# Half products in the last group of the down projection, and one first load for norm weights and x

## The chip, the cores and the metric

The kernel runs on one core of a Trainium2 chip. Its time is in device microseconds, as the median of several executions. A core has TensorE (matmuls; PE in the profile), VectorE (DVE), ScalarE (ACT), GpSimd (POOL) and SyncE (SP). SP, ACT and POOL also issue DMAs; a DMA that POOL issues can add what it carries to what stands at its destination. "PEld" is TensorE's loading of a weight tile, "PEclk" the clock that the chip grants to TensorE.

## The reference

One decoder layer over 512 tokens of width 1024 in float32: a pooling mixer and a sparse attention side by side, joined by gates, then a feed-forward network with a causal convolution of width 3. Cut to what matters here:

```python
h = rms_norm(x, mix_norm_g)
proj = h @ w_in                                     # u, q, kv, gates
# kv's first two slots go, block by block, into compressed keys and values:
blk = kv[:, idx] + pe                               # additive position weights
hid = silu(einsum('bnlgd,ldh->bngh', blk, w1));  kc = hid @ w2
x = x + (gate_pool * y_pool + gate_nsa * y_nsa) @ w_out
h = rms_norm(x, ffn_norm_g)
gate_pre, val = split(h @ w_up)                     # 2 x 2816 features
y = silu(causal_dwconv(gate_pre, conv_w, conv_b)) * val
x = x + y @ w_down                                  # 2816 -> 1024
```

## The kernel before

Activations stand transposed, 128 features in the partitions and 512 tokens along the row. A float32 matrix product is made of three matmuls: each operand is split into a rounded high part and a low remainder (`split`: ScalarE copies the high part, VectorE subtracts; `split_by_dma` leaves the subtraction to a POOL DMA that adds), and high x high, high x low and low x high are summed in a PSUM bank (`mm3`).

The order is not written out. Every operation is recorded by `Plan.note`, with what it reads and writes. `Plan.emit` then tries several orders with rough costs of its own, and issues the best: each engine's queue in the order found. TensorE's own order is that of the program, in two streams that are interleaved during the attention. `pl.behind(op)` holds an operation back until another one is done; `soon` tiles are handed out in the order of the program. Recorded operations all carry the line at which `emit` issues them, so the profile names nearly everything L394; tiles tell what an instruction is.

Tiles are drawn from a common set of 54 pages of 512 columns (`page`), from rings of three for raw and split weights (`wraw`, `whi`, `wlo`, 1024 columns each) and from PSUM banks (`mm`, `tr`, `av`, `sc`); `any_bank` walks over them.

The stages that the change touches:

- **The head.** `first` loads the first weights `wa[0]` in two parts over SP's queue, and between them the first half of the first x tile; ScalarE's queue loads sixteen columns of the parameters (`pr`, among them the norm weights `mixg`) and then the other half of x. ScalarE scales x by the norm weight into `xh`. Until then TensorE runs nine warm-up matmuls on ones. The remaining parameters come after the second round of this stage.
- **Compression.** `kv_in` makes `kc`, and VectorE adds the position weights to give `kcb`; these additions are `behind(turned[3])`, the last operation that is recorded for the last of the four transposed query and key tiles (`qk_transpose`: TensorE transposes, ScalarE and VectorE copy into `qt` and `kt`). TensorE multiplies `kcb` with `w1`, and the result goes as `hid` into a small matmul with `w2`.
- **The up projection** runs over 22 features f, each a gate and a value tile. Features 0 and 2 are made plainly (`up_plain`), the others by `up_fast`: the four blocks of output (gate and value by two halves of 256 tokens) come from seven half products instead of eight, on sums of weights and of activations (`product`, twelve matmuls of 256 columns each). The last two products of a feature are `held` and run within the next one.
- **The down projection** is in groups of four features of y. When four are ready (`AT`), a group puts eight blocks of twelve matmuls of 512 columns on a list (`dn_group`), and `FILL` says how many of them each later feature takes between its products (`fill`). What is left runs after the last feature. Its sums stay in `x2`.
- **The last group** takes the six features y[16] to y[21]: for each of the eight output tiles f, weights `wdz[f]` (768 columns), eighteen matmuls of 512 columns, an addition of `x2[f]` and the output. The last tile goes in two halves of 256 tokens.

```python
    for f in range(8):
        wh, wl = weights(flat(wdz[f]), 768, "v")
        pt = any_bank()
        o = page("o")
        if f < 7:
            mm3(pt, wh, wl, yh, yl, 16, KF, koff=16, nk=KF, first=16)
            DVE.tensor_add(o, pt, x2[f])
            SP.dma_start(out[f], o)
            continue
        # the last tile: the same in two halves of 256 tokens
```

Of the kernel before, what the change touches and what calls it, by code (L numbers as in the profile page):

```python
# [57 lines left out]
FILL.update({18: (0, 1, 0, 0), 19: (0, 1, 0, 0), 20: (0, 1, 0, 0), 21: (0, 1, 0, 0)})  # L58
# [339 lines left out]
def hybrid_layer(ctx: ExitStack, tc: tile.TileContext, xT, pos, par, cst, poolw, w1, wa, wb, wf,  # L398
# [71 lines left out]
    pr = keep("pr", (P, NPAR))  # L470
    ps_i = keep("ps_i", (P, 5), I32)
# [17 lines left out]
    mixg = R("mixg")  # L489

    POOL.memset(ones, 1.0)
    ACT.dma_start(pr[:, 0:16], par[:, 0:16])
    pt = bank("mm")
    for i in range(9):
        PE.matmul(pt[:, 0:P], ones, ones, start=(i == 0), stop=(i == 8))
# [7 lines left out]
    H2 = T // 2  # L503

# [4 lines left out]
    def first():  # L509
        raw, hi, low = ring("wraw"), ring("whi", F32R), ring("wlo", F32R)  # L510
        xr[0] = page("xr")
# [8 lines left out]
        DVE.tensor_copy(hi[:, :T], raw[:, :T])  # L520
        for c in cuts:
# [53 lines left out]
    for k in range(KD):  # L575
# [12 lines left out]
        if k == 1:  # L588
            SP.dma_start(ps_i, pos)
            SP.dma_start(cs, cst)  # L590
            SP.dma_start(pr[:, 16:], par[:, 16:])
# [110 lines left out]
    def qk_transpose(t):  # L702
# [7 lines left out]
        if t % 2:  # L710
            pt = bank("tr", (P, 2, 2, P))
            with pl.unit():
                for j in range(2):
                    for b in range(2):
                        PE.transpose(pt[:, j, b], kp[t - 1 + j][:, 2 * b:2 * b + 2].rearrange("p a d -> p (a d)"), ident)
            for g in range(2):
# [8 lines left out]
    turned = []  # L725
# [20 lines left out]
    with pl.on("f"):  # L746
        def kv_in(i):
# [417 lines left out]

    def split_y(f, y):
        yh[f], yl[f] = page("yh", dt=F32R), page("yl", dt=F32R)
        split(yh[f], yl[f], y)

# [26 lines left out]
    def product(bank_, a, b, k0):  # L1196
        ah, al = a
        bh, bl = b
        for k in range(4):
            c = slice(k * P, (k + 1) * P)  # L1200
            with pl.unit():
                for j, (w, x) in enumerate(((ah, bh), (ah, bl), (al, bh))):
                    PE.matmul(back(bank_[:, :H2]), w[:, c], back(x(k)), start=k0 and k == 0 and j == 0,
                              stop=k == 3 and j == 2, skip_group_check=True)
# [41 lines left out]
    def up_fast(f, n1, n2, n3):  # L1246
        rg, r1, r2 = ring("wraw"), soon("r1"), soon("r2")
        SP.dma_start(rg, flat(wup[f, 0]))
        with pl.behind(begun[-2 - max(0, 3 - f)]):
            SP.dma_start(r1, flat(wup[f, 1, :, 0:4]))  # L1250
            SP.dma_start(r2, flat(wup[f, 1, :, 4:8]))

        def pair():
            return soon("sh", F32R), soon("sl", F32R)

        def summed(x):
            lo, hi = soon("sl", F32R), soon("sh", F32R)
            split_by_dma(hi, lo, x)
            return hi, lo

        a1 = ring("whi", F32R), ring("wlo", F32R)
        split(*a1, rg)
        halves_ = lambda a, i: tuple(q[:, i * 512:(i + 1) * 512] for q in a)
        s3 = soon("s3")
        DVE.tensor_add(s3, rg[:, :512], r1)
        h5 = summed(r2)
        DVE.tensor_add(r1, r1, r2)
        h3 = summed(s3)
        DVE.tensor_add(rg[:, :512], rg[:, :512], r1)
        h1 = summed(r1)  # L1270
        h2 = pair()
        split(*h2, rg[:, :512])
        DVE.tensor_add(rg[:, 512:], rg[:, 512:], rg[:, :512])
        h4 = summed(rg[:, 512:])
# [4 lines left out]
        product(bx, halves_(a1, 0), mov(0, 0), True)  # L1279
# [16 lines left out]
        product(bx, halves_(a1, 1), mov(1, 0), False)  # L1296
# [32 lines left out]
    for f in range(8):  # L1329
# [3 lines left out]
        if f < 7:  # L1333
            mm3(pt, wh, wl, yh, yl, 16, KF, koff=16, nk=KF, first=16)
            DVE.tensor_add(o, pt, x2[f])
            SP.dma_start(out[f], o)
            continue
        for h in range(2):
            s = slice(h * H2, (h + 1) * H2)
            pt = any_bank() if h else pt  # L1340
            for k in range(16, KF):
                c = slice((k - 16) * P, (k - 15) * P)
                with pl.unit():
                    for j, (w, q) in enumerate(((wh, yh), (wh, yl), (wl, yh))):
                        PE.matmul(back(pt[:, :H2]), w[:, c], back(q[k][:, s]), start=k == 16 and j == 0,
                                  stop=k == KF - 1 and j == 2)
            DVE.tensor_add(o[:, s], pt[:, :H2], x2[f][:, s])
            SP.dma_start(out[f, :, s], o[:, s])
# [4 lines left out]
_INS = ["xT", "pos", "par", "cst", "poolw", "w1", "wa", "wb", "wf", "wpo", "wno", "wout", "wup", "wdn", "wdz"]  # L1353


def _layout(x, positions, mix_norm_g, w_in, q_norm_g, k_norm_g, cmp_pe, cmp_w1, cmp_w2, pool_w,
# [30 lines left out]
    A["par"] = np.concatenate([par[n] for n in PAR], axis=1)  # L1387
    q, kk = np.arange(P)[:, None], np.arange(P)[None, :]
# [55 lines left out]
```

## Time and profile before

| | |
|---|---|
| median of 3 runs | 691.0 us (690.94 to 691.12) |
| profiled execution | 690.67 us, its span 688.9 us |
| TensorE, its weight loads | 683.1 us (99%), 606.0 us (88%) |
| VectorE, ScalarE, POOL | 502.6 (73%), 430.0 (62%), 100.2 (15%) |
| granted clock | 1.0 throughout |
| moved by DMA | 113.99 MB, 165 GB/s on average |

Times in the profile count from the span's start. A timeline's row gives start, duration, engine, operation, what it writes and reads, the count, and in brackets the idle time before it with what ended it. Matmuls overlap: the duration of one (0.39 us for 512 columns) is longer than the distance to the next. A group's row gives the count, busy time and the mean in ns of one, and idle time; a DMA group's row the size and the median from issue to landing. A row of a stretch gives its length and then for TensorE, weight loads, VectorE, ScalarE and POOL the busy time and (count), then the granted clock, the share of the DMA engines and GB/s.

### The profile page before, as it was taken

The page shows a single profiled execution, that of the slowest core. Times are in us where ns is not written, and L with a number is a line of the kernel's source. Part 1 is how long each engine was busy: PE and PEld are TensorE (multiplying, and loading weights), DVE is VectorE, ACT ScalarE, POOL GpSimd, SP SyncE. Part 2 cuts the span into 40 slices and gives each one's busy share as a digit, 9 for nine tenths or more (in the row PEclk, how much of TensorE's full clock was granted, in tenths as well). Part 3 has the DMA queues.
Part 4 walks back from the last instruction along what each step waited for, and adds up shares of the span by engine and source line. Part 5 has one row for each costly group of instructions (what it writes and reads, how often), then busy time and mean ns, then how long its engine had stood idle before and what let it go on. Part 6 is the DMA issues. An engine that isn't in the chain of part 4 may idle for free.

```text
span 688.9 us, 11345 instructions
## 1 busy us (share of the span) xinstructions
PE 683.1 (99%) x4126; PEld 606.0 (88%) x4126; DVE 502.6 (73%) x1093; ACT 430.0 (62%) x781; POOL 100.2 (15%) x126
## 2 busy tenths in 40 slices
PE   9999999999999999999999999999999999999997
PEld 8898888888888888888898999999999999999976
DVE  6868678887877644768868978677778777786642
ACT  7667477776776653346778866666567656675320
POOL 0011210111111110001123332122213222211000
PEclk9999999999999999999999999999999999999999
DMA  8468653545545557844778889677668667765131
GB/s 301 143 165 264 154 121 94 139 100 145 154 123 154 153 138 246 279 148 154 209 167 221 199 180 218 154 199 184 153 170 185 170 157 194 170 167 115 47 130 61
DMA packets 46279, 113.99 MB, mean 165 GB/s; under 512 B 5392, under 2 KB 6160, under 8 KB 46224
## 3 DMA queue, kind: packets, MB, share of 16 engines
q1 hardware_dynamic: 29808, 76.43, 32.5%
q0 software_dynamic: 16128, 36.71, 29.9%
q8 instruction: 32, 0.52, 0.3%
q14 instruction: 23, 0.19, 0.1%
q10 hardware_dynamic: 288, 0.14, 0.1%
HBM read 70.27 MB, written 6.29 MB: 111 GB/s over the span
## 4 chain that ended last, share of the span: by engine, by line
PE 97%; DVE 1%; DMA 1%; ACT 0%; issue 0%; SPq 0%
PE mm L394 37%; PE tr L394 33%; PE sc L394 16%; PE av L394 11%; DMA wraw<-wa 1%; ACT kt L394 0%; DVE ft L394 0%; DVE fg L394 0%; DVE wlo L394 0%; ACT ft L394 0%; SPq L394 0%; DVE yl L394 0%; DVE kcb L394 0%; DVE u L394 0%; DVE kt L394 0%
## 5 line engine op out<-in xcount | busy, mean ns | idle before, releaser
L394 ACT ACTIVATE whi<-wraw 128x1024 fp32r<-128x1024 f32 (+2 forms) x94 | 95.2, 1015 | 65.8 <-PE mm L394 26.7
L394 DVE TENSOR_TENSOR wlo<-wraw,whi 128x1024 fp32r<-128x1024 f32 (+1 forms) x66 | 76.2, 1156 | 4.6 <-ACT whi L394 4.2
L394 PE MATMUL mm<-xh,whi 128*128 128x512 f32 x176 | 72.3, 411 | 0.1
L394 PE MATMUL tr<-tl,sh 128*128 128x256 f32 x250 | 70.4, 282 | 0.0
L394 PE MATMUL mm<-xh,wlo 128*128 128x512 f32 x176 | 68.9, 392 | 0.0
L394 PE MATMUL mm<-xl,whi 128*128 128x512 f32 x176 | 68.9, 391 | 0.0
L394 PE MATMUL tr<-th,sl 128*128 128x256 f32 x240 | 67.7, 282 | 0.0
L394 PE MATMUL tr<-th,sh 128*128 128x256 f32 x240 | 67.5, 281 | 0.0
L394 PE MATMUL mm<-gh,whi 128*128 128x256 f32 (+1 forms) x320 | 60.8, 288 | 0.0
L394 POOL DMA_DIRECT2D wlo<-wraw x28 | 24.3, 867 | 238.3 <-ACT wlo L394 182.0
L394 POOL DMA_DIRECT2D sl<-r x40 | 34.5, 862 | 134.2 <-ACT sl L394 98.0
L394 PEld LDWEIGHTS mm<-gh,whi 128*128 128x128 f32 x320 | 49.5, 188 | 0.6
L394 PEld LDWEIGHTS tr<-tl,sh 128*128 128x128 f32 x250 | 47.0, 188 | 0.5
L394 PE MATMUL sc<-yh,whi 128*128 128x512 f32 x120 | 46.7, 389 | 0.0
L394 PE MATMUL sc<-yl,whi 128*128 128x512 f32 x120 | 46.7, 389 | 0.0
L394 PE MATMUL sc<-yh,wlo 128*128 128x512 f32 x120 | 46.7, 389 | 0.0
L394 PEld LDWEIGHTS tr<-th,sh 128*128 128x128 f32 x240 | 45.2, 188 | 1.2
L394 PE MATMUL mm<-gh,wlo 128*128 128x256 f32 (+1 forms) x160 | 45.9, 287 | 0.0
L394 PEld LDWEIGHTS tr<-th,sl 128*128 128x128 f32 x240 | 45.1, 188 | 0.0
L394 DVE SCALAR_TENSOR_TENSOR ft<-fg,pr,ft 128x511 f32<-128x511 f32 (+1 forms) x44 | 32.9, 749 | 14.3 <-ACT ft L394 13.7
L394 PEld LDWEIGHTS mm<-xh,wlo 128*128 128x128 f32 x176 | 33.0, 188 | 7.5
L394 ACT ACTIVATE u<-tr 128x256 f32<-128x256 f32 x40 | 15.3, 384 | 36.8 <-PE tr L394 24.2
(380 smaller groups left out, 1927.2 us busy)
## 6 DMA issues: line engine op xcount, KB each, us to landing
wlo<-wraw POOLq DMA_DIRECT2D x28, 512.0 KB, 4.7
wraw<-wup SPq DMA_DIRECT2D x24, 512.0 KB, 3.6
wraw<-wf SPq DMA_DIRECT2D x22, 512.0 KB, 3.4
r<-wup SPq DMA_DIRECT2D x40, 256.0 KB, 3.5
sl<-r POOLq DMA_DIRECT2D x40, 256.0 KB, 4.0
wraw<-wdn SPq DMA_DIRECT2D x16, 512.0 KB, 3.7
sl<-s POOLq DMA_DIRECT2D x20, 256.0 KB, 4.3
sl<-wraw POOLq DMA_DIRECT2D x20, 256.0 KB, 4.3
```

Source lines behind the costliest of these rows:

```text
L394: getattr(self.real[o.eng], method)(*a, **kw)
```

## The change

Four edits:

1. **The last group.** Output tiles 0 and 1 stay plain. Tiles 2 to 7 go in pairs (f, e) through `dz_fast`: seven products, each of three k x three matmuls of 256 columns, for two tiles by two halves of tokens. `y_sums` makes the sums and differences of y that this needs, for k = 16 to 18 with k + 3, when y[k + 3] is there. `half_weights`, taken out of `up_fast`, makes the sums of weights, at width 384 here. Three of its five halves are split with a POOL DMA, two by VectorE. `dz_plain` is the loop's body as it was.
2. **The fills.** `FILL` takes none of the blocks within features 19, 20 and 21; the three run after the last feature, in front of the last group.
3. **Compression.** The additions of `kcb` are behind the last transposition of keys on TensorE instead of behind the last copy of the tile.
4. **The head.** A new input `xa` has the sixteen parameter columns in front of the first x tile. ScalarE's queue loads the parameters and the first half of x in one DMA, SP's the second half. x and `mixg` then lie in `x0`, in the space that `ptc` takes later. `xl` is made in two halves; there are eight warm-up matmuls; the parameters are loaded whole later.

```diff
-FILL.update({18: (0, 1, 0, 0), 19: (0, 1, 0, 0), 20: (0, 1, 0, 0), 21: (0, 1, 0, 0)})
+FILL.update({18: (0, 1, 0, 0), 19: (0, 0, 0, 0), 20: (0, 0, 0, 0), 21: (0, 0, 0, 0)})
...
+    x0 = pl.tile(sb, (P, 4, T), F32, "x0", "ptc", 1).rearrange("p a t -> p (a t)")
...
-    mixg = R("mixg")
+    mixg = x0[:, 48:56]
...
-    ACT.dma_start(pr[:, 0:16], par[:, 0:16])
+    ACT.dma_start(x0[:, 48:64 + H2], xa[:, :16 + H2])
...
-    for i in range(9):
+    for i in range(8):
...
             SP.dma_start(raw[:, :T], wa[0, :, :T])
-            SP.dma_start(xr[0][:, cuts[0]], xT[0, :, cuts[0]])
+            SP.dma_start(xr[0][:, cuts[1]], xa[:, 16 + H2:])
             SP.dma_start(raw[:, T:768], wa[0, :, T:768])
-        ACT.dma_start(xr[0][:, cuts[1]], xT[0, :, cuts[1]])
...
-        DVE.scalar_tensor_tensor(xl[0], xr[0], mixg[:, 0:1], f32(xh[0]), op0=ALU.mult, op1=ALU.subtract)
+        for c in cuts:
+            with pl.behind(cast):
+                DVE.scalar_tensor_tensor(xl[0][:, c], xr[0][:, c], mixg[:, 0:1], f32(xh[0][:, c]), op0=ALU.mult,
+                                         op1=ALU.subtract)
...
-                with pl.behind(turned[3]):
+                with pl.behind(flipped[1]):
...
+    def y_sums(k):
+        b1, b2 = ylast[k], ylast[k + 3]
+        ta, tb = page("ta"), page("tb")
+        DVE.tensor_sub(ta[:, :H2], b1[:, :H2], b1[:, H2:])
+        DVE.tensor_sub(tb[:, :H2], b2[:, H2:], b1[:, H2:])
+        DVE.scalar_tensor_tensor(ta[:, H2:], ta[:, :H2], -1.0, b2[:, H2:], op0=ALU.mult, op1=ALU.subtract)
+        DVE.scalar_tensor_tensor(tb[:, H2:], ta[:, H2:], -1.0, b2[:, :H2], op0=ALU.mult, op1=ALU.subtract)
+        for i, x in ((0, ta), (1, tb)):
+            yth[k - 16, i], ytl[k - 16, i] = page("yth", dt=F32R), page("ytl", dt=F32R)
+            split(yth[k - 16, i], ytl[k - 16, i], x)
...
+    def half_weights(first, second, w, dma, gate):
+        rg, r1, r2 = ring("wraw"), soon("r1"), soon("r2")
+        SP.dma_start(rg[:, :2 * w], first)
+        with pl.behind(gate):
+            SP.dma_start(r1[:, :w], second[0])
+            SP.dma_start(r2[:, :w], second[1])
...
+        a1 = tuple(ring(n, F32R)[:, :2 * w] for n in ("whi", "wlo"))
+        split(*a1, rg)
+        s3 = soon("s3")[:, :w]
+        DVE.tensor_add(s3, rg[:, :w], r1)
+        h5 = parts(r2, dma[0])
+        DVE.tensor_add(r1, r1, r2)
+        h3 = parts(s3, dma[1])
+        DVE.tensor_add(rg[:, :w], rg[:, :w], r1)
+        h1 = parts(r1, dma[2])
+        h2 = parts(rg[:, :w], dma[3])
+        DVE.tensor_add(rg[:, w:], rg[:, w:], rg[:, :w])
+        h4 = parts(rg[:, w:], dma[4])
...
+    DZ = (True, True, False, False, True)
+
+    def dz_fast(f, e):
...
+        bx, by, bq = any_bank(), any_bank(), any_bank()
+        of, oe = page("o"), page("o")
+        product(bx, a11, ymov(0, 0), True, 3)
+        begun.append(pl.last())
+        ACT.activation(by[:, L], bx[:, L], AF.Copy)
+        product(bq, h1, ymov(2, 0), True, 3)
+        DVE.tensor_sub(oe[:, Rr], x2[e][:, Rr], bq[:, L])
+        product(by, h2, ymov(2, 1), False, 3)
+        DVE.tensor_add(of[:, Rr], by[:, L], x2[f][:, Rr])
+        product(bx, a12, ymov(1, 0), False, 3)
+        DVE.tensor_add(of[:, L], bx[:, L], x2[f][:, L])
+        SP.dma_start(out[f, :, L], of[:, L])
+        product(by, h3, ymov(3, 0), False, 3)
...
+        product(bq, h4, ymov(1, 1), False, 3)
...
+        product(by, h5, ymov(3, 1), False, 3)
+        DVE.tensor_sub(oe[:, L], x2[e][:, L], by[:, L])
+        SP.dma_start(out[e, :, L], oe[:, L])
+
+    for f in range(2):
+        dz_plain(f)
+    for f in range(2, 8, 2):
+        dz_fast(f, f + 1)
```

More of the change, by code (lines that the diff above doesn't have):

```diff
@@ L1194, in back, with product @@
         return bass.AP(tensor=x.tensor, offset=x.offset + n - 1, ap=[list(x.ap[0]), [-1, n]])
[L1196 removed]
+    def product(bank_, a, b, k0, n=4):
         ah, al = a
         bh, bl = b
[L1199 removed]
+        for k in range(n):
             c = slice(k * P, (k + 1) * P)
@@ L1328, in hybrid_layer, with ymov, dz_plain @@
     fill(9, True)
-    for f in range(8):
+    def ymov(i, half):
+        c = slice(half * H2, (half + 1) * H2)
+        if i < 2:
+            return tuple((lambda k, q=q: q[16 + 3 * i + k][:, c]) for q in (yh, yl))
+        return tuple((lambda k, q=q: q[k, i - 2][:, c]) for q in (yth, ytl))
+    def dz_plain(f):
         wh, wl = weights(flat(wdz[f]), 768, "v")
@@ L1332, in hybrid_layer @@
         o = page("o")
[L1333 to L1348, printed above, removed]
+        mm3(pt, wh, wl, yh, yl, 16, KF, koff=16, nk=KF, first=16)
```

75 lines of the change are left out of this document (40 added, 35 removed).

## The prediction

> **What bounds the kernel now.** I read the page first, then the waits of TensorE, then the timeline at the places they name.
>
> ```profile
> span 688.9 us, 11345 instructions
> PE 683.1 (99%) x4126; PEld 606.0 (88%) x4126; DVE 502.6 (73%) x1093; ACT 430.0 (62%) x781; POOL 100.2 (15%) x126
> PE 97%; DVE 1%; DMA 1%; ACT 0%; issue 0%; SPq 0%
> PE mm L394 <- POOL ones L394: 1.0, 1, 1.0
> PE tr L394 <- DVE kcb L394: 0.6, 1, 0.6
> PE tr L394 <- ACT xh L394: 0.3, 1, 0.3
> PE av L394 <- DVE yl L394: 0.2, 1, 0.2
> ```
>
> TensorE is busy 683.1 of 688.9 us, the chain that ended last is TensorE for 97%, and in the whole span it waits four times that the view of waits can name. So a gain is either TensorE work removed, priced by the distance from one matmul's start to the next, or one of these waits. Everything else is cover, and the question is whether it holds.
>
> **The last group's products.** The distances come from the timeline of the eight features of that group.
>
> ```profile
> 656.47 0.39 PE L394 MATMUL mm<-yh,whi 128*128 128x512 f32 x1
> ...
> 680.73 0.39 PE L394 MATMUL av<-yh,wlo 128*128 128x512 f32 x1
> 680.96 0.28 PE L394 MATMUL mm<-yh,whi 128*128 128x256 f32 x1
> ...
> 685.10 0.28 PE L394 MATMUL tr<-yh,wlo 128*128 128x256 f32 x1
> ```
>
> From 656.47 to 680.73 stand features 1 to 6 without a gap: 6 x 18 matmuls of 512 columns, 24.26 us over 107 steps, 226.7 ns each. Feature 7 is in two halves, 36 matmuls of 256 columns: 4.14 us over 35 steps, 118.3 ns each. A narrow one costs 5 ns more than half a wide one.
>
> The change leaves features 0 and 1 as they are and makes 2 to 7 in three pairs of seven products, a product being 3 x 3 matmuls of 256 columns. Before: 5 features x 18 x 226.7 ns = 20.40, and 36 x 118.3 ns = 4.26, together 24.66 us. After: 3 x 63 = 189 x 118.3 ns = 22.36 us. **Gain 2.30 us**, a ninth of the work less what narrow matmuls cost more.
>
> The Trainium skill (TensorE: Matmul & The Clock Gate, section Back-to-back issue gap) gives an isolated warm gap of N/2.4 + 2.5 ns, that is 216 and 109 ns here; an estimate by it would make this gain 2.7 us. The spacing in the trace is larger for both widths, and the sum goes by the trace.
>
> **The wait for the last y.** Three of four FILL entries are dropped, so that three more 12-matmul blocks of the group before come behind the last round: four instead of one.
>
> ```profile
> 654.77 0.39 PE L394 MATMUL av<-yh,wlo 128*128 128x512 f32 x1
> 655.16 0.49 PE L394 MATMUL av<-yh,whi 128*128 128x512 f32 x1
> 655.89 0.50 PE L394 MATMUL av<-yl,whi 128*128 128x512 f32 x1 [0.23 <-DVE yl L394]
> 656.23 0.40 PE L394 MATMUL av<-yh,wlo 128*128 128x512 f32 x1
> ```
>
> From 654.77 to 656.23 there are three steps in 1.46 us, at 226.7 ns each 0.68: 0.78 us is lost because the last k of feature 0 stands ready for hi and lo of the last y. Afterwards feature 0 starts three blocks, 3 x 12 x 226.7 ns = 8.16 us, further behind that y. **Gain 0.78 us.** What is late next is the sums and differences of y that the pairs need (below).
>
> **The held additions.** `kcb` is held today until the last copy of transposed keys is queued; the change holds it only until TensorE's last key transposition.
>
> ```profile
> 70.81 0.60 PE L394 MATMUL tr<-cs,kp 128*128 128x128 f32 x4
> ...
> 73.77 0.39 PE L394 MATMUL mm<-xh,wlo 128*128 128x512 f32 x1
> 74.75 3.90 PE L394 MATMUL tr<-kcb,w 128*128 128x62 f32 x32 [0.59 <-DVE kcb L394]
> 70.55 0.68 DVE L394 TENSOR_TENSOR qt<-tr,qt 64x512 fp32r<-64x512 f32 x1
> 72.67 0.69 DVE L394 TENSOR_TENSOR kt<-tr,kt 64x512 fp32r<-64x512 f32 x1 [1.44 <-ACT kt L394]
> 73.29 0.69 DVE L394 TENSOR_TENSOR qt<-tr,qt 64x512 fp32r<-64x512 f32 x1
> 74.00 1.29 DVE L394 TENSOR_TENSOR kcb<-kc,pr 128x512 f32<-128x512 f32 x2
> ```
>
> TensorE could start its `kcb` matmuls at 73.77 + 0.23 = 74.00 and starts at 74.75. VectorE idles 1.44 us before `kt` and does `kt`, `qt`, then `kcb`. In the new order `kcb` stands right behind the two `qt`: 70.55 + 2 x 0.6 = 71.75, after the transposition that begins at 70.81, done at 73.05. The wait of 0.75 goes; `kt` comes later, but nobody reads it before the scores. New is that both small `hid` matmuls now stand one triple (0.68 us) behind the second compression, where the second stood two behind; I take 0.1 back. **Gain 0.65 us** (bounds: none, if `qt` waits for ScalarE as `kt` does; 0.75).
>
> **The head.**
>
> ```profile
> 0.74 0.41 ACTq L394 DMA_DIRECT2D pr<-par  x1
> 0.99 3.63 PE L394 MATMUL mm<-ones 128*128 128x128 f32 x18 [0.99 <-POOL ones L394]
> 1.17 0.45 ACTq L394 DMA_DIRECT2D xr<-xT  x1
> 1.65 4.10 DMA wraw<-wa
> 4.34 0.91 ACT L394 ACTIVATE xh<-xr,pr 128x256 fp32r<-128x256 f32 x2 [1.19 <-DMA xr<-xT]
> 4.90 0.97 PE L394 MATMUL tr<-whi,xh 128*128 128x512 f32 x3 [0.27 <-ACT xh L394]
> 5.77 0.42 ACT L394 ACTIVATE whi<-wraw 128x256 fp32r<-128x256 f32 x1 [0.52 <-DMA wraw<-wa]
> 6.24 0.74 PE L394 MATMUL sc<-whi,xh 128*128 128x256 f32 x4
> ```
>
> One load of ScalarE's queue takes the place of two, so half of x leaves at 0.74 instead of 1.17, and `xh` can begin up to 0.43 us earlier. But TensorE waits a second time: `sc` at 6.24 needs the last weight columns, which SP issues at 1.65 and which land at 5.75. That DMA keeps its place in SP's queue and carries the same bytes; it gains only what the 128 tiny rows of `pr` cost and what is moved earlier. The bounds are 0.45 gained and 0.2 lost (the weights now share the engines earlier); I take **0.15**, near nothing, because the wait behind is unchanged. Dropping a ninth warm-up matmul is hidden: the eighteen records end 0.27 us before `tr`, and two fewer end 0.4 earlier.
>
> **What must hold as cover.** VectorE and ScalarE have more to make than now: sums of y (per k four operations of 256 columns and two splits of 512), and for each pair four weight sums and six splits, three of which go as accumulations of 192 KB through POOL's queue. And rounds 19 to 21 lose their fills, so that each lasts 7 x 12 x 118.3 ns = 9.94 us. Two stretches (TensorE, its loads, VectorE, ScalarE, POOL, clock, DMA share, GB/s), a group of DMAs and the timeline of VectorE:
>
> ```profile
> 357.90:383.00 25.10, 25.10 (x170) 23.23 (x170) 20.59 (x32) 19.58 (x35) 6.90 (x8) 1.00 0.92 222
> 605.30:643.30 38.00, 38.00 (x290) 36.60 (x289) 28.41 (x48) 22.28 (x39) 5.17 (x6) 1.00 0.51 120
> sl<-r POOLq DMA_DIRECT2D x40, 256.0 KB, 4.0
> 609.09 0.41 DVE L394 TENSOR_TENSOR y<-y,rb 128x256 f32<-128x256 f32 x1
> 609.42 0.68 DVE L394 TENSOR_TENSOR wraw<-wraw 128x512 f32<-128x512 f32 x1
> 610.02 0.68 DVE L394 TENSOR_TENSOR yl<-y,yh 128x512 fp32r<-128x512 f32 x1
> ```
>
> The first row is a stretch of such rounds without fills that exists already: VectorE 20.59 of 25.10, ScalarE 19.58, the DMA engines 92%, and TensorE full. So the round as such holds. In the stretch of rounds 19 to 21 VectorE has 28.41 us; without three fill additions (2.1) and with the first y sums (2.8) it is 29 for the 29.8 us that three short rounds last, so it is nearly full, and order decides. I counted VectorE's new order down from the rows, 0.33 us from start to start for 256 columns and 0.60 for 512. TensorE's side, by the clock of the profile before: rounds at 605.3, 615.3 and 625.2, their end at 635.2, five fill blocks of 2.72 and two products of 1.42 until 651.6, two plain features until 659.8, then pairs of 7 x 1.065 = 7.45 us. The tightest places: round 21 multiplies by `h2` third, due at 625.2 + 2 x 1.42 + 0.24 = 628.3, and VectorE has its low half at 627.0; the y differences are due with pair one's second product at 660.8 and are done at 657.5; ScalarE's copy of the first product from bank to bank is done at 661.4, due at 661.9; pair three's loads stand behind two output DMAs in SP's queue, land at about 667, and their halves are due at 675.7. POOL's accumulations take 4.0 us to land; round 21's are issued by 623 and due from 630.9 on. All hold, two by little. I set **0.25 us** against small new waits.
>
> The end stays: after the last matmul one 256-column addition and one 128 KB output, as now.
>
> **Sum.** 2.30 + 0.78 + 0.65 + 0.15 - 0.25 = 3.6 us. The profiled execution took 690.67 us (span 688.9 and 1.77 around it), 0.3 below the median of 691.0; so 687.1 against itself and 687.4 against the median.
>
> **Rivals.**
> - *Cover breaks in places.* Six preparations are new in kind (three rounds, three pairs). The two waits of this kind in the trace cost 0.75 and 0.78 us; if three of six wait so, 2.1 are lost: 689.5. For it speaks a VectorE at 29 of 29.8 us; against it the stretch at 357.90 with TensorE full.
> - *The gate falls at the start.* The warm-up's 18 records of 128 columns take 3.63 us, 202 ns each; the four of 128 columns at 70.81 take at most 150. So TensorE begins slowly, and with the warm-up over at 4.2 its first work could go at that pace once more: another 3.63 us so lose at least 3.63 x (1 - 150/202) = 0.9, and half of it, 1.8, at half speed; by the worse end 689.2. Against it: the idle time before `tr` is 0.27 us today and 0.4 more at most. The Trainium skill (TensorE: Matmul & The Clock Gate, Part 1) puts the clock back only after an idle window of about 3.4 us, which speaks against this rival too.
> - *Narrow matmuls are bound by their weight load, and the time is slower.*
>
> ```profile
> L394 PEld LDWEIGHTS tr<-tl,sh 128*128 128x128 f32 x250 | 47.0, 188 | 0.5
> ```
>
> A load takes 188 ns whatever the columns. Were that the step, 189 x 188 ns = 35.5 us against 24.66: 10.9 lost, 1.3 gained elsewhere, 700.6. It decides from (24.66 + 1.33)/189 = 137.5 ns a step; feature 7 runs at 118.3 with a load for each matmul, so only new operands could bring it there. The Trainium skill (same page and section) gives sustained 81 ns at 128 columns and 131 at 512; a straight line through them is an estimate of 98 at 256, by which splitting would lose 3.2 us. The trace has 226.7 where it says 131, so I give this little.
> - *The held additions stay late* (`qt` behind ScalarE): 688.1, inside the first case's range.
>
> **Chances.** Forecast, with the last rival in it, 0.80; cover breaks 0.13; gate 0.03; weight load 0.04. 0.2% is 1.4 us, about what can be told from no change, so faster means below 689.6. The forecast and the gate lie there, and half of "cover breaks" (0.06): faster 0.89; same 0.06; slower 0.05. The range reaches from 686.4 (a head gain of 0.45, `kcb` 0.75, no new waits, and 0.3 for the profile being below its median) to 689.3, which takes in the gate and the nearer half of the broken cover.
>
> **What would show it.** Right: 189 matmuls of 256 columns at 118 ns in the last 23 us; no wait for `yl` or `kcb` in TensorE's view of waits; `sc` of the head still behind its weights near 6 us; the span near 685.3. Wrong: waits of TensorE for `sl`, `ytl` or a bank copy behind 615 us, or steps of the pairs over 130 ns.

## The result, and the profile after

The changed kernel takes 687.86 us (median of 6 runs, 687.01 to 688.69) against 691.06 (690.79 to 691.15) for the kernel before. The ratio on record is 0.9939, with a 95% interval of 0.9917 to 0.9962; the two medians by themselves give 0.9954. Its profiled execution took 687.27 us with a span of 685.5, so the span is 3.40 us shorter.

The page of the changed kernel, and its view of TensorE's waits:

```profile
span 685.5 us, 11622 instructions
PE 680.7 (99%) x4187; PEld 607.8 (89%) x4187; DVE 518.8 (76%) x1138; ACT 443.4 (65%) x811; POOL 108.0 (16%) x135
PE 97%; DMA 1%; DVE 1%; ACT 0%; issue 0%; POOL 0%; POOLq 0%
PE mm L394 <- POOL ones L394: 1.0, 1, 1.0
PE tr L394 <- DVE qp L394: 0.6, 1, 0.6
```

TensorE bounds the kernel as before. Its waits for `kcb`, `xh` and `yl` are gone; one for `qp` is new.

To see where the 3.40 us come from, the span is cut at three places that both kernels have: A, the first transposition of q; B, the first matmul on `gh`; C, the last matmul. TensorE's timeline, before and then after:

```profile
9.59 0.39 PE L394 MATMUL tr<-whi,xh 128*128 128x512 f32 x1
30.39 0.95 PE L394 MATMUL mm<-ones,acc 128*128 128x1 f32 x8
53.45 0.60 PE L394 MATMUL tr<-cs,qp 128*128 128x128 f32 x4
342.14 0.62 PE L394 MATMUL av<-gh,whi 128*128 128x512 f32 x2
```

```profile
4.57 1.65 PE L394 MATMUL tr<-whi,xh 128*128 128x512 f32 x3
6.01 0.57 PE L394 MATMUL av<-whi,xh 128*128 128x512 f32 x1
6.42 0.64 PE L394 MATMUL sc<-whi,xh 128*128 128x256 f32 x4
9.72 0.40 PE L394 MATMUL tr<-whi,xh 128*128 128x512 f32 x1
30.93 0.50 PE L394 MATMUL mm<-ones,acc 128*128 128x1 f32 x4
53.99 0.60 PE L394 MATMUL tr<-cs,qp 128*128 128x128 f32 x4
66.55 0.39 PE L394 MATMUL mm<-xh,wlo 128*128 128x512 f32 x1
67.56 0.63 PE L394 MATMUL tr<-cs,qp 128*128 128x128 f32 x4 [0.61 <-DVE qp L394]
342.32 0.62 PE L394 MATMUL av<-gh,whi 128*128 128x512 f32 x2
659.89 0.28 PE L394 MATMUL tr<-yh,whi 128*128 128x256 f32 x1
682.13 0.28 PE L394 MATMUL av<-yth,sl 128*128 128x256 f32 x1
```

| stretch | before | after | gained |
|---|---|---|---|
| start to A (head, projections) | 53.45 | 53.99 | -0.54 |
| A to B (compression, attention and more) | 288.69 | 288.33 | 0.36 |
| B to C (feed-forward, last group) | 342.96 | 339.81 | 3.15 |
| C to the end of the span | 3.79 | 3.36 | 0.43 |

The pairs run from 659.89 to 682.13, 22.24 us over 188 steps of 118.3 ns, without a gap. So the last group did what was forecast. The total of 3.6 came nearly true as well, but two of the smaller rows are of the other sign or size than forecast, and the last row was not forecast at all. The experiments went after those.

### The profile page after: what moved, and what is told of

The parts are those of the page before. It is cut to its first block, busy times and chain, and to the rows that moved or that the text cites. A ratio compares the mean times of both kernels' runs of the same rounds, so it can differ in the third digit from the quotient of the medians.

```text
span 685.5 us, 11622 instructions
## 1 busy us (share of the span) xinstructions
PE 680.7 (99%) x4187; PEld 607.8 (89%) x4187; DVE 518.8 (76%) x1138; ACT 443.4 (65%) x811; POOL 108.0 (16%) x135
## 4 chain that ended last, share of the span: by engine, by line
PE 97%; DMA 1%; DVE 1%; ACT 0%; issue 0%; POOL 0%; POOLq 0%
PE mm L394 37%; PE tr L394 34%; PE sc L394 14%; PE av L394 12%; DMA w<-w 1%; ACT kt L394 0%; DVE qp L394 0%; DVE qt L394 0%; ACT wlo L394 0%; DVE u L394 0%; DVE kt L394 0%; DVE o L394 0%; DVE rt L394 0%; POOL ones L394 0%; POOLq L1490 0%
## 5 line engine op out<-in xcount | busy, mean ns | idle before, releaser
L394 ACT ACTIVATE whi<-wraw 128x1024 fp32r<-128x1024 f32 (+2 forms) x91 | 92.7, 1019 | 41.8 <-PE mm L394 16.1
L394 DVE TENSOR_TENSOR wlo<-wraw,whi 128x1024 fp32r<-128x1024 f32 (+1 forms) x63 | 73.3, 1165 | 5.8 <-ACT whi L394 4.1
L394 POOL DMA_DIRECT2D sl<-r x43 | 37.1, 862 | 161.9 <-ACT sl L394 90.8
L394 PE MATMUL sc<-yh,whi 128*128 128x512 f32 x108 | 42.2, 390 | 0.0
L394 PE MATMUL sc<-yl,whi 128*128 128x512 f32 x108 | 42.0, 389 | 0.0
L394 PE MATMUL sc<-yh,wlo 128*128 128x512 f32 x108 | 42.0, 389 | 0.0
L394 ACT ACTIVATE wlo<-wraw 128x1024 fp32r<-128x1024 f32 x28 | 29.7, 1060 | 15.9 <-PE mm L394 12.9
```

The source lines that it names most:

```text
L394: getattr(self.real[o.eng], method)(*a, **kw)
```

## The experiments

The runs were made on four chips in four groups (experiments 1 to 4; 5, 6, the fills of 7 and the first run of 9; the rest; the last), each beside runs of the kernel before, to which the ratios stand. Single executions scatter by some us there, of the kernel before too (689.8 to 695.6 in the first group). A time therefore can't carry a question of 0.4 us; the stretches behind A can, since they repeat within 0.05 us where nothing waits. A itself can't: it lies anywhere from 52.49 to 54.41 with the same head. The table is told row by row below. "Late" is by how much the steps in front of matmuls on `sh` and `sl`, the weight halves, last longer than the same steps in an undisturbed profile; it is taken out of B to C. (In "rotation freed" B to C still holds 1.5 us of steps at half pace, in "last group only" A to B holds 3.16; both are explained below.)

| kernel | median us | A | A to B | B to C less late | late | C to end |
|---|---|---|---|---|---|---|
| before | 691.06 | 53.45 | 288.69 | 342.96 | 0 | 3.79 |
| whole change | 687.86 | 53.99 | 288.33 | 339.81 | 0 | 3.36 |
| last group only | 688.56 | 54.30 | 291.85 | 339.88 | 0.89 | 3.79 |
| head only | 690.97 | 53.13 | 288.71 | 343.01 | 0.96 | 3.35 |
| held additions only | 692.41 | 53.84 | 288.37 | 342.97 | 1.51 | 3.79 |
| nine warm-ups | 688.36 | 52.80 | 288.31 | 339.82 | 1.55 | 3.37 |
| whole change again | 688.38 | 52.49 | 288.30 | 339.81 | 0 | 3.37 |
| rotation freed | 687.73 | 54.41 | 287.14 | 341.29 | 4.96 | 3.37 |
| first load split | 689.66 | 53.80 | 288.33 | 339.82 | 0.49 | 3.80 |
| fills kept | 688.11 | 53.57 | 288.33 | 340.37 | 0.68 | 3.37 |
| pairs undone | 690.00 | 54.08 | 288.31 | 342.15 | 1.65 | 3.35 |
| old hold | 688.44 | 54.00 | 288.69 | 339.81 | 0.79 | 3.38 |
| rotation freed again | 687.61 | 53.26 | 287.14 | 339.82 | 1.21 | 3.37 |
| first sum held | 686.16 | 52.91 | 287.58 | 339.81 | 0 | 3.37 |

**1. The last group alone** (against the kernel before):

```diff
-FILL.update({18: (0, 1, 0, 0), 19: (0, 1, 0, 0), 20: (0, 1, 0, 0), 21: (0, 1, 0, 0)})
+FILL.update({18: (0, 1, 0, 0), 19: (0, 0, 0, 0), 20: (0, 0, 0, 0), 21: (0, 0, 0, 0)})
+    for f in range(2, 8, 2):
+        dz_fast(f, f + 1)
```

> Only the last group is changed (pairs of half products, sums of y, fills dropped); the head and the held additions stay as before. The prediction's theory: the last y's wait goes (0.78) and the narrow products save 2.30, so the last matmul starts 3.1 us earlier than before and the time is about 688.0 us, 3.1 below the kernel before (with up to 0.4 more if the last output's transfer is shorter too, as in the changed kernel). Rival, from the changed kernel's trace: the other two parts cost something between them (0.18 us by 342 us), so this kernel is as fast as or faster than the whole change, 687.3 to 688.0. If the other parts are worth the 0.8 predicted, the whole change is 0.8 faster than this one.

Measured: 688.56 us, ratio to the kernel before 0.9966 (0.9941 to 0.9990). B to C is 339.88, the whole change's value: the last group brings its 3.1 us by itself. The head is the old one, and so is the end, 3.79: the shorter end does not belong to the last group's outputs. The rival, that the other two parts cost something between them, can't be told by these times, and the rows of A to B and of the end speak against it. This profile also has something that the others do not; TensorE's timeline and the stretches (TensorE, its loads, VectorE, ScalarE, POOL, clock, DMA share, GB/s):

```profile
75.60 4.59 PE L394 MATMUL tr<-kcb,w 128*128 128x62 f32 x32 [0.59 <-DVE kcb L394]
79.95 0.77 PE L394 MATMUL mm<-xh,whi 128*128 128x512 f32 x1
80.52 0.63 PE L394 MATMUL mm<-xl,whi 128*128 128x512 f32 x1
75.02:78.43 3.41, 2.83 (x25) 2.83 (x26) 3.31 (x7) 3.36 (x5) 1.58 (x4) 1.00 0.55 172
78.43:85.25 6.82, 6.82 (x23) 5.66 (x22) 4.01 (x9) 1.06 (x3) 1.33 (x6) 0.50 0.63 147
```

At 78.43 us, 2.8 us after the wait for `kcb` has ended, the granted clock falls to 0.50 and stays there for 6.8 us; the 512-column steps in it last 427 ns. A to B is 3.16 longer for it. The last section comes back to this.

**2. The head alone** (against the kernel before):

```diff
-    ACT.dma_start(pr[:, 0:16], par[:, 0:16])
+    ACT.dma_start(x0[:, 48:64 + H2], xa[:, :16 + H2])
-    for i in range(9):
+    for i in range(8):
-        ACT.dma_start(xr[0][:, cuts[1]], xT[0, :, cuts[1]])
```

> Only the head is changed (norm weights in front of the first x tile, one load for both, eight warm-up matmuls). The prediction's theory: 0.15 us faster (0.45 faster to 0.2 slower). Rival A, clock at the start: the spacing of TensorE's matmuls stays at 213 ns until about 6 us instead of falling to 108 at 3.7 us, the four first products of 512 columns step at 427 ns, and 'sc' starts near 6.4 instead of 6.24. Rival B, cadence: from 10 to 31 us a pair of steps (512 and 256 columns) takes 353.3 ns instead of 346.7, 60 pairs, 0.4 us, for a reason that lies in the phase at which the stage begins. With both, 0.5 us slower than before by 31 us. If neither shows here, the loss in the whole change came from its other parts.

Measured: 690.97 us, ratio 0.9994 (0.9974 to 1.0015). ScalarE and TensorE at the start:

```profile
3.96 0.91 ACT L394 ACTIVATE xh<-x 128x256 fp32r<-128x256 f32 x2 [1.28 <-DMA x<-xa]
4.78 0.40 ACT L394 ACTIVATE whi<-wraw 128x256 fp32r<-128x256 f32 x1
5.55 0.64 PE L394 MATMUL sc<-whi,xh 128*128 128x256 f32 x4
```

Rival A did not show: the steps are short from about 4.5 us on. `xh` begins at 3.96 instead of 4.34, and `sc` follows at 5.55 instead of 6.24, since the last weight columns were there early too. Rival B did show: the pair of steps takes 353.3 ns from 10 to 31 us. Both together leave A 0.32 earlier. And the end is 3.35: the shorter end belongs to the head.

**3. The held additions alone** (against the kernel before):

```diff
+            flipped.append(pl.last())
-                with pl.behind(turned[3]):
+                with pl.behind(flipped[1]):
```

> Only the hold of the compression's additions is changed. The prediction's theory: TensorE's wait of 0.75 us for kcb at 74 us goes and nothing takes its place: 0.65 us faster, 690.4 us. Rival, from the changed kernel's trace: the wait goes, but the planner's new order puts a 'kt' product, which waits for ScalarE, ahead of the 'qp' chain on VectorE, and TensorE waits about 0.78 us at 66 us for qp instead: net 0, 691.0 us. If the kcb wait goes and no wait shows near 66 us, the new order in the whole change comes from the head's other instructions.

Measured: 692.41 us, ratio 1.0011 (0.9990 to 1.0032). A to B is 288.37, 0.32 less than before; the wait for `kcb` is gone and TensorE loses 0.77 us in front of the last q transposition, as in the whole change. The rival holds for the two waits, which cancel. What is gained lies elsewhere, in 0.41 us of steps of narrow matmuls. The two `hid` pairs now stand together, and their four steps take 375 ns instead of 517. No `hid` matmul stands right behind the compression any more: the step there took 225 ns, and takes 48 in front of a wide matmul. The first compression step, which came out of the wait, takes 93 ns instead of 179. The times do not show the gain: the interval has 1 in it, and the twelve runs lie between 690.3 and 696.3.

**4. Nine warm-up matmuls** (against the whole change):

```diff
-    for i in range(8):
+    for i in range(9):
```

> The whole change with nine warm-up matmuls (18 records) instead of eight. If the number of warm-up matmuls holds TensorE's clock, the spacing falls from 213 to 108 ns by 3.7 us again, the first products step at 230 ns, and the time is 0.2 to 0.6 us below the whole change. If the moment of the fall is set by a window that runs apart from the kernel's work, the moment varies from run to run in both kernels and the times are the same within 0.3 us, with two groups of times 1.4 us apart in either kernel.

Measured: 688.36 us, ratio 0.9950 (0.9932 to 0.9969). TensorE's start:

```profile
1.00 4.21 PE L394 MATMUL mm<-ones 128*128 128x128 f32 x18 [1.00 <-POOL ones L394]
4.86 1.12 PE L394 MATMUL tr<-whi,xh 128*128 128x512 f32 x3
5.82 0.39 PE L394 MATMUL av<-whi,xh 128*128 128x512 f32 x1
```

The steps become short near 5.2 us. With as many warm-ups the kernel before had them short at 3.9, and the last group alone only at 6.7. The number of warm-ups does not set the moment. The two groups of times that the expectation has with it did not show: the twelve runs are spread from 686.4 to 690.5.

**5. The whole change again**, unaltered.

> The whole change once more, unaltered. If the moment at which TensorE's clock rises and the cadence of the projections (346.7 or 353.3 ns for a step pair of 512 and 256 columns) belong to the kernel, the clock again rises near 6.1 us, a pair takes 353.3 ns, and the first q transposition starts at 54.0 us. If they belong to the single execution, these differ here: a rise anywhere from 3.7 to 6.5 us, and that milestone between 52.8 and 54.3. Fixed in either case: the last group free of waits, 682.13 - 342.32 = 339.8 us from the first matmul on gh to the last one (plus any wait for a weight half that POOL's queue delivers late), the wait of 0.78 us for qp near 67 us, and 3.36 us from the last matmul to the end.

Measured: 688.38 us, ratio 0.9962 (0.9948 to 0.9976). TensorE in the profile:

```profile
9.31 0.40 PE L394 MATMUL tr<-whi,xh 128*128 128x512 f32 x1
30.11 0.95 PE L394 MATMUL mm<-ones,acc 128*128 128x1 f32 x8
52.49 0.60 PE L394 MATMUL tr<-cs,qp 128*128 128x128 f32 x4
340.79 0.61 PE L394 MATMUL av<-gh,whi 128*128 128x512 f32 x2
680.60 0.28 PE L394 MATMUL av<-yth,sl 128*128 128x256 f32 x1
```

The same kernel reaches A 1.50 us earlier than in its first profile: 0.41 by 9.31 us (clock), 0.41 by 30.11 (20.80 us for the stretch instead of 21.21), and 0.68 up to A, most of it because 95 steps of 280 columns last 129 ns each instead of 134. Everything behind A is the same to 0.03 us. So the head's -0.54 in the first comparison was of that execution and not of the kernel.

**6. The first load split in two** (against the whole change):

```diff
-    ACT.dma_start(x0[:, 48:64 + H2], xa[:, :16 + H2])
+    ACT.dma_start(x0[:, 48:64], xa[:, :16])
+    ACT.dma_start(x0[:, 64:64 + H2], xa[:, 16:16 + H2])
```

> The whole change, but the norm weights and the first half of x are loaded by two transfers on ScalarE's queue, as before. Theory of the end: the 0.43 us between the two ends (3.79 us from the last matmul's start to the end of the span with the old head, 3.36 with the new) comes from the number of transfers before the last output, which decides at which place of the closing list of semaphores the last output stands; one transfer more puts it back to 3.79 although the last group is the same. Rival: the end is shorter because of the last group's outputs (it was not: the head alone has 3.35 too) or because of the head's timing; then it stays at 3.36. For the head: if the one load is what brings x early, the first product starts up to 0.43 later than with one load (4.57 to 4.9) whenever the warm-up leaves it free to.

Measured: 689.66 us, ratio 0.9980 (0.9961 to 0.9998). C to the end is 3.80 again, and `xh` begins late, so that the first product starts at 4.96 us (4.53 to 4.86 in the ten profiles with one load):

```profile
4.39 0.91 ACT L394 ACTIVATE xh<-x 128x256 fp32r<-128x256 f32 x2 [1.24 <-DMA x<-xa]
682.44 0.28 PE L394 MATMUL av<-yth,sl 128*128 128x256 f32 x1
span 686.2 us, 11624 instructions
```

The closing instructions of SP show why. SP waits for nine pairs of semaphores of transfers in a fixed order, about 0.06 us each. In the kernel before the pair that the last output signals is the second: it is done 1.3 us before the span's end, and seven others are still to be asked. In the changed kernel it is the ninth, at 0.88 us before the end, and the eight others have been asked meanwhile. One load more, as here, puts the last output back to the second place. In all 14 profiles the end is 3.79 or 3.80 with two early loads on ScalarE's queue (four profiles), 3.35 to 3.38 with one (ten). The median is 1.28 us above that of the whole change beside it (688.38), of which the end explains 0.43; the runs reach from 686.82 to 692.96, and the rest is open.

**7. Fills kept, and pairs undone** (each against the whole change):

```diff
-FILL.update({18: (0, 1, 0, 0), 19: (0, 0, 0, 0), 20: (0, 0, 0, 0), 21: (0, 0, 0, 0)})
+FILL.update({18: (0, 1, 0, 0), 19: (0, 1, 0, 0), 20: (0, 1, 0, 0), 21: (0, 1, 0, 0)})
```

> The whole change with the three dropped fills kept: one block of the group before is left behind the last round instead of four. The prediction's theory: the last y comes 8.16 us later against the pairs. The wait for yl at 656 us (0.78) comes back, and the differences of y, done at 657.5 by the prediction's count against a due time of 660.8, are 8.16 later and so 4.9 us too late: together a loss of up to 5 us against the whole change. Rival: VectorE has more room in the filled rounds and the planner moves the sums forward, so that only the 0.78 comes back.

Measured: 688.11 us, ratio 0.9956 (0.9941 to 0.9972). The waits of 5 us did not come:

```profile
656.00 0.50 PE L394 MATMUL av<-yl,whi 128*128 128x512 f32 x1 [0.21 <-DVE yl L394]
659.75 0.68 DVE L394 TENSOR_TENSOR ytl<-tb,yth 128x512 fp32r<-128x512 f32 x1
```

TensorE waits for `yl` once more, and B to C is 0.56 longer. The last low half of the y sums is begun at 659.75: the planner had brought the sums close behind the last y, so that the pairs do not wait. The rival holds, with 0.56 in place of 0.78.

```diff
-    for f in range(2):
-        dz_plain(f)
-    for f in range(2, 8, 2):
-        dz_fast(f, f + 1)
+    for f in range(8):
+        wh, wl = weights(flat(wdz[f]), 768, "v")
...
-        if f > 18:
-            y_sums(f - 3)
```

> The whole change, but the eight features of the last group are made as before (seven wide, the eighth in two halves, no sums of y); the three fills stay dropped. This parts the two terms of the last group. The prediction's theory: from the first matmul on gh to the last matmul it was 342.96 us before and is 339.81 with the whole change (without waits for weight halves that POOL's queue delivers late); here the wait for the last y is gone (0.78) and the narrow products' 2.30 are not there, so 342.2 us. Rival, from the kernel with its fills kept, which lost only 0.5 us by its wait for yl: the dropped fills are worth 0.5 and the pairs 2.65; then 342.45.

Measured: 690.00 us, ratio 0.9977 (0.9962 to 0.9992). B to C is 342.15, as the theory has it: dropping the fills is worth 342.96 - 342.15 = 0.81 us, the pairs 342.15 - 339.81 = 2.34. With the pairs the fills are worth 0.56, since the steps around the wait for `yl` lose 0.49 us there instead of 0.78.

**8. The old hold** (against the whole change):

```diff
-                with pl.behind(flipped[1]):
+                with pl.behind(turned[3]):
```

> The whole change with the compression's additions held as before. The stretch from the first q transposition to the first matmul on gh was 288.69 us before and is 288.33 and 288.30 in the two profiles of the whole change; theory: the old hold gives the 0.75 us wait for kcb back and takes the 0.78 us wait for qp away, and the stretch is 288.7. Second question, the granted clock: the runs of the three kernels with the kcb wait (before, last group only, head only) had a mean clock of 0.994 or 0.995 in 20 of 95 runs, each some 3.5 us longer; those without that wait (six kernels, 73 runs) in none. If that wait, followed by matmuls of 62 columns, is what brings the clock down, some 2 or 3 of 12 runs here are at 0.995 and near 691.5; if it is the chip or the day, none more than in the others.

Measured: 688.44 us, ratio 0.9943 (0.9921 to 0.9965). A to B is 288.69 and the wait is back:

```profile
75.30 0.59 PE L394 MATMUL tr<-kcb,w 128*128 128x62 f32 x3 [0.59 <-DVE kcb L394]
```

So the hold is worth 0.36 to 0.39 us in the stretch. The second question stays open here: none of the 7 runs was at 0.995.

**9. The rotation freed** (against the whole change). The new wait comes from VectorE, whose timeline has this `kt` in the kernel before and these rows in the whole change:

```profile
60.94 0.69 DVE L394 TENSOR_TENSOR kt<-tr,kt 64x512 fp32r<-64x512 f32 x1 [1.45 <-ACT kt L394]
```

```profile
63.20 0.69 DVE L394 TENSOR_TENSOR kt<-tr,kt 64x512 fp32r<-64x512 f32 x1 [1.46 <-ACT kt L394]
63.92 0.69 DVE L394 TENSOR_TENSOR qp<-av,small 128x512 f32<-128x512 f32 x1
64.64 1.39 DVE L394 TENSOR_TENSOR qt<-tr,qt 64x512 fp32r<-64x512 f32 x2
66.07 0.29 DVE L394 TENSOR_TENSOR qp<-qp,gq 128x128 f32<-128x128 f32 x1
```

`kt` stands about 1.45 us for ScalarE in both, but it begins 9.21 us behind A instead of 7.49. The last `qp` can only come behind it: its rotation is held, as the additions were, until a last copy of transposed keys, here those of the first two tiles.

```diff
-            with pl.behind(turned[t]):
+            with pl.behind(flipped[0] if t == 1 else turned[t]):
                 rotate(t + 2)
```

> The whole change, and the rotation of the last query tile is held only until the key transposition on TensorE instead of until the last copy of the transposed keys. Theory: the wait of 0.78 us for qp at 66.5 us is the held rotation (on VectorE it stands behind a kt product that waits 1.46 us for ScalarE), so it goes and nothing takes its place: the stretch from the first q transposition to the first kcsp transposition becomes 0.78 shorter than the whole change's 38.26 us, 37.5, and the time 0.78 less than the whole change's. Rival: the wait moves on once more, to kp at the next transpositions or to kcb, as the hold's change moved it from kcb to qp; then the stretch stays at 38.0 to 38.3 us.

Measured: 687.73 us, ratio 0.9954 (0.9936 to 0.9972). From A to the first `kcsp` transposition it is 37.45 us instead of 38.26; the wait is gone and none takes its place. A to B is 1.16 us shorter than in the second profile of the whole change, because a step of 0.48 us at 127.7, and a long one behind it, went too. This profile has the largest late steps of all, 4.96 us, and shows where they come from in the rounds that the change leaves alone (ScalarE, then TensorE):

```profile
466.22 0.64 ACT L394 ACTIVATE sl<-r 128x512 fp32r<-128x512 f32 x1 [4.94 <-DMA r<-wup]
471.96 0.36 ACT L394 ACTIVATE u<-tr 128x256 f32<-128x256 f32 x1
472.38 0.39 PE L394 MATMUL tr<-th,sh 128*128 128x256 f32 x1 [1.76 <-ACT u L394]
```

A load of weights on SP's queue lands late, ScalarE stands 4.94 us and works off the splits first, and its copy of a bank, for which TensorE waits, comes too late. The expectations put this down to POOL's queue; here it is a load. Of the ten profiles in which TensorE waits so for `u`, ScalarE's longest wait in the 12 us before is for such a load in six (3.2 to 4.9 us) and for a transfer of POOL's queue in three (1.9 to 3.6 us); in the head alone it is for neither. It falls in different rounds in different executions, with the old last group too.

> The kernel with the freed rotation once more, beside the two above. The stretch from the first q transposition to the first matmul on gh was 287.14 us there against 288.30 in the whole change; if that is the kernel's and not the single execution's, it is 287.1 again, with no wait of TensorE between 60 and 130 us, and the time is 0.6 to 1.2 below the whole change and 3 to 4 below the kernel before. Rival: the part behind 92 us (0.35 of the 1.16) was chance, and the stretch is 287.5.

Measured: 687.61 us, ratio 0.9931 (0.9907 to 0.9955); A to B is 287.14 again, so both parts of the 1.16 are the kernel's.

**10. The first sum of y held** (against the freed rotation). The late steps have one place that belongs to the change. VectorE and TensorE in the profile with nine warm-ups:

```profile
624.35 0.43 DVE L394 TENSOR_TENSOR ta<-y 128x256 f32<-128x256 f32 x1 [2.04 <-DMA sl<-r]
624.69 1.53 DVE L394 SCALAR_TENSOR_TENSOR ft<-fg,pr,ft 128x511 f32<-128x511 f32 x2
627.94 0.68 DVE L394 TENSOR_TENSOR sl<-wraw,sh 128x512 fp32r<-128x512 f32 x1
628.67 0.39 PE L394 MATMUL tr<-th,sl 128*128 128x256 f32 x1 [0.56 <-DVE sl L394]
```

A new y sum stands 2.04 us for a transfer of POOL's queue, and behind it on VectorE is round 21's half `h2`, for which TensorE waits. In five of the eight profiles with the new last group and the dropped fills 0.7 to 1.0 us were lost between 627 and 634 us: in three of them the sum waits like this (1.92 to 2.22 us) and TensorE waits for `sl`. In two the `ft` behind it waits 1.96 and 1.99 us for ScalarE, which has itself stood 1.92 and 2.31 us for a transfer of POOL's queue, and most of the loss is TensorE's wait for a bank copy `u`. In the other three the sum waits 0.47 to 0.72 us and nothing is lost.

```diff
-        if f > 18:
+        if f > 19:
             y_sums(f - 3)
+        if f == 21:
+            with pl.behind(low2[-1]):
+                y_sums(16)
```

(`low2` collects the low half of `h2` of each round.)

> The kernel with the freed rotation, and the first sums of y (k = 16) are held on VectorE behind the split of round 21's weight half h2. Theory: in five of eight profiles with the new last group TensorE waits 0.7 to 1.0 us in rounds 20 or 21 for sl, because VectorE, in program order, has a new sum of y or the operation behind it in front of that split and stands up to 2.2 us there for a transfer of POOL's queue (or for ScalarE behind one); with the sums behind the split no wait of TensorE shows between 625 and 636 us, and from the first matmul on gh to the last one it is 339.8 us plus only what waits of the earlier rounds cost. Rival: the split is late because its own operands are late (POOL's transfers take 4.8 to 5.2 us here instead of 4.0); then the wait of 0.7 to 1.0 stays in more than half of the profiles, this one as likely as not. For the time: up to 0.6 below the kernel with the freed rotation alone (687.7), 3.5 to 4.5 below the kernel before.

Measured: 686.16 us (685.43 to 686.78), ratio 0.9921 (0.9900 to 0.9942), the lowest median of all, and no wait of TensorE behind 342 us. But this does not test the theory, since the edit held another sum than the one that waits. Each `ta<-y` needs one y alone, that of its k. The profile with nine warm-ups has three of them, at 598.58, 609.39 and 624.35, for k = 16, 17 and 18. Here that of k = 16 has moved from the first place to the end, to 626.35; that of k = 18 stands where it stood, and in this execution it had nothing to wait for.

```profile
621.56 0.42 DVE L394 TENSOR_TENSOR ta<-y 128x256 f32<-128x256 f32 x1
624.81 0.69 DVE L394 TENSOR_TENSOR sl<-wraw,sh 128x512 fp32r<-128x512 f32 x1
626.35 0.42 DVE L394 TENSOR_TENSOR ta<-y 128x256 f32<-128x256 f32 x1
```

That the waiting sum delays `h2` stays argued, not shown. The lower median has no reason in the stretches: B to C is the undisturbed 339.81, and A to B is 0.44 longer than with the freed rotation alone, as the planner also parted the `hid` pairs again. The interval overlaps that of the freed rotation (0.9907 to 0.9955).

## Why the prediction was right, and where it was not

The time forecast, 687.4, and the time measured, 687.86, lie within half a us, by these steps:

- **The pairs, 2.30:** right; 2.34 measured, with the same steps of 118.3 ns. The weight-load rival is out: there is no step of 137.5 ns.
- **The wait for the last y, 0.78:** right for the reason given; 0.81 without the pairs. The step behind it, that the y differences would be the next to be late, did not hold: with the fills kept they should have cost up to 5 us and cost none.
- **The held additions, 0.65:** the step that failed is "the wait of 0.75 goes" with nothing but 0.1 taken back. The wait went, and one of 0.78 came seven us earlier. The prediction said that `kt` comes later and that nobody reads it before the scores. It overlooked that the last rotation is held behind the copies of the first transposed keys: their `kt` came 1.7 us later, and `qp` with it. What remains, 0.36, comes from the narrow matmuls put together, for which the sum took 0.1 off.
- **The head, 0.15:** mis-sized, and the reason was wrong. `sc` does not always wait behind its weights. In the kernel before it does: their copy ends at 6.19 and `sc` starts at 6.24. In the whole change the copy ends at 5.86, and `sc` starts at 6.42 only because the four products in front of it step at half pace; so the sign named for being right, `sc` behind its weights near 6 us, did not come. `xh` begins at 4.13 us on average in the ten profiles with the one load and at 4.29 in the three with the old head, 0.16 earlier. More depends on when TensorE's steps become short, which differs by 2.9 us from execution to execution, and on the pace of the projections, which alone moves A by up to 1.1 us. A mean over the three old heads (53.86) and the ten new ones (53.46) favours the new by 0.4, inside a spread of 1.9: not settled. The rival "the gate falls at the start" named a slow start that exists, but ascribed it to idle time; it needs none.
- **The end, "as now":** wrong by 0.43, gained. The prediction counted the addition and the output and not SP's list of waits behind it.
- **The reserve of 0.25 for new waits:** not used in the profiled execution; in five of eight 0.7 to 1.0 was lost, in three of them at a place called tight, the low half of `h2` in round 21, and in two mostly at a bank copy beside it. "Cover breaks in places" is therefore part of what happens, in some executions and in one place of six.

So 2.30 + 0.78 carried the result, 3.15 measured, and the errors of the rest (-0.69 at the head, -0.29 at the additions, +0.43 at the end, +0.25 unused) nearly cancelled. That they did was luck: the largest of them belongs to one execution.

## What to carry to other kernels

Price removed matmuls by the distance between starts in that very kernel, and check it with the part undone: it holds to hundredths of a us. When a hold is loosened, look for other work held by the same kind of event, since the wait moves there; freeing both was worth four times as much as freeing one (1.55 us against 0.36 to 0.39). Before calling a difference of half a us at the start of a kernel an effect, profile the same kernel twice.

## What the runs showed of the hardware

**The start of TensorE is of the execution.** Its warm-up steps last 213 ns until some moment between 3.84 and 6.75 us in the 14 profiles, with eight or nine warm-ups and the same kernel alike. At that moment the traces' records of the granted clock begin, so the 1.0 that the views show ahead of it stands for no record. Within a trace the later changes of the clock lie whole multiples of 3.413 us from this first one (71.68 us is 21 of them and 6.83 is 2 in the last group alone, 467.63 is 137 with the rotation freed). The Trainium skill (TensorE: Matmul & The Clock Gate, Part 1) has the window of the clock gate run free of the kernel, 3.4 us long, so that the moment varies, by 0.5 us either way. The traces agree with the window and not with the 0.5: the moments lie 2.9 us apart. The prediction used only the other half of that rule.

**Two cadences.** A step pair of 512 and 256 columns takes either 346.7 or 353.3 ns on average throughout a stretch of 60 pairs (20.80 or 21.21 us), in the same kernel. What chooses is not settled.

**A short wait can bring the clock down.** In the kernels whose TensorE waits 0.75 us for `kcb` and goes on with 62-column matmuls, 27 of 131 executions had a mean granted clock of 0.994 or 0.995 and took some 3.5 us longer (19 of 100 of the kernel before); in those without that wait 0 of 97, though four of these had 0.997 or 0.998. A fall like the profiled one, half the clock for 6.83 us, costs 3.4 us, which is 0.005 of the span. That the wait is the cause is not shown: the kernel with only the old hold had none in 7. The Trainium skill (same page and part) asks for an idle window of about 3.4 us before the clock falls. Neither of the two falls that the traces show ahead of the kernel's end had that. In the last group alone the 3.41 us before the fall hold 2.83 us of busy TensorE (the rows in experiment 1), and with the rotation freed, around a wait of 1.76 us, they hold 1.65:

```profile
470.16:473.57 3.41, 1.65 (x14) 1.45 (x14) 3.11 (x6) 3.41 (x7) 1.41 (x2) 1.00 0.79 123
473.57:476.99 3.42, 3.42 (x12) 2.84 (x11) 3.24 (x7) 1.87 (x4) 0.86 (x1) 0.50 0.72 195
```

Counted in such windows from each trace's first record, the first fall follows the window with the fewest matmul columns of all 14 profiles ahead of their ends (1550; the nearest without a fall is the old hold's, with 1612), the second the window with the least busy time (the nearest without a fall has 2.34 us). So it may be chance, by where the windows lie, whether the wait for `kcb` and the narrow matmuls share one; two falls do not show it.

**The place of the last output in the closing list is worth 0.43 us** here, and one early transfer more or less decided it.
